# The up projection of a feed-forward layer as a Strassen product of halves, with weight sums made by accumulating transfers

## The chip, the cores and the metric

The kernel runs on one core of one Trainium2 chip. A core has five engines with an instruction stream each: TensorE (PE, matrix products, with its weight loads shown as PEld), VectorE (DVE), ScalarE (ACT), GpSimd (POOL) and SyncE (SP, which here issues most of the DMA transfers). They meet at semaphores. Operands lie in SBUF, products accumulate in PSUM, weights come from HBM by DMA. The metric is the device time of one execution in microseconds; the time before is the median of three runs.

## The reference, cut to what matters

One layer of a hybrid block: a mixer (HGRN2 and mLSTM heads), a residual with layer norm, cross-attention to a memory, a residual with layer norm (LN2), a feed-forward part with a causal convolution, a residual with layer norm. 512 tokens, width 1024, feed-forward width 2816, all in float32. The change lies in the feed-forward part:

```python
def conv_ffn(x, w_up, conv_w, conv_b, w_down):
    u = causal_dwconv(x @ w_up, conv_w, conv_b)     # 512x1024 @ 1024x5632, then 3 taps along the tokens
    gate, val = jnp.split(u, 2, axis=-1)
    return (jax.nn.gelu(gate) * val) @ w_down
...
        x = layer_norm(ALPHA * x + ca, ln2_g[l], ln2_b[l])
        ff = conv_ffn(x, ffn_w_up[l], ffn_conv_w[l], ffn_conv_b[l], ffn_w_down[l])
        x = layer_norm(ALPHA * x + ff, ln3_g[l], ln3_b[l])
```

## The kernel before

Every large product is made in three passes: each float32 operand is split on the chip in a high part (a cast to the matmul format) and a low part (the rest), and `mm3` (L153 to L156) issues high by high (L154), high by low (L155) and low by high (L156) into one PSUM bank. `split` (L118 to L126) splits a block of weights 128 x 1024: a cast on ACT (`wh`, L124), a subtraction on DVE (`wl`, L125), in four buffers each.

The order of work on PE, ACT and DVE is set by a planner inside the kernel's framework, which orders each engine's stream by the program order and its estimate of what is ready; the engines then run their streams in that order, and wait at semaphores. GpSimd and SyncE work in the order in which the instructions are written.

The part before the up projection is the second half of the product with `ca_wo` (by `slab`). For each of four token blocks it adds the residual (`resid`, L658, with the statistics at L660), normalizes (LN2: L664, L422 and L423 for the inverse root, L671 and L673) and transposes the block (`transpose_block`, L252 on PE, then a split out of PSUM: cast at L243 on ACT, subtraction at L244 on DVE) into `x2h` and `x2l`. The transposes of the last block are held back (`x2_last`).

The up projection runs over 22 pairs, each a tile of 128 gate columns and the tile of 128 value columns that belongs to it. A tile is `col_tile`: eight steps along the width by three passes, 24 matmuls with 512 tokens as columns. The first two pairs (`early`) run in two halves of 256 tokens, with `x2_last` between them, so that PE has work on the first tokens while LN2 of the last block ends. `ffn_finish` takes a pair's two banks: `conv3` (a scaled copy with bias on ACT at L793, two DVE operations at L795 for the other taps), the gelu (L802), gate times value (L803), and the split of the result into `hTh` and `hTl` (L804 on ACT, L805 on DVE). The down projection is `slab` twice over the 22 k steps, two at a time, for four token blocks each, and ends with LN3 and the stores.

Names in the profile are those of the tiles: `raw` is a block of weights as loaded, `wh` and `wl` its parts, `fc` a convolved tile, `mm` and `mx` PSUM banks.

## Time and profile before

| | us |
|---|---|
| median of three runs | 819.92 (819.73 to 820.85) |
| the profiled execution | 819.77 |
| its span, first to last instruction | 818.1 |
| its mean granted TensorE clock | 0.995 of full |
| up projection, from its first matmul | 448.57 to 690.00 |
| down projection | 690.00 to 811.00 |
| end (LN3 and stores) | 811.00 to 818.10 |

The span is cut in stretches by the first matmul of each stage. In a view by windows a row gives the stretch, its length, the busy time of PE, PEld, DVE, ACT and POOL with the number of instructions, the granted clock of TensorE, the share of time in which the 16 DMA engines worked, and GB/s. In a timeline a row gives the start, the duration, engine, line, operation, and what it writes from what; a matmul's duration overlaps the next one's, so the length of a step is the distance of two starts. In a view by groups the numbers behind the bar are the busy time of all, the mean of one in ns, and the idle time before them with its releaser.

### The profile page before, as it was taken

The page shows a single profiled execution, that of the slowest core. Times are in us where ns is not written, and L with a number is a line of the kernel's source. Part 1 is how long each engine was busy: PE and PEld are TensorE (multiplying, and loading weights), DVE is VectorE, ACT ScalarE, POOL GpSimd, SP SyncE. Part 2 cuts the span into 40 slices and gives each one's busy share as a digit, 9 for nine tenths or more (in the row PEclk, how much of TensorE's full clock was granted, in tenths as well). Part 3 has the DMA queues.
Part 4 walks back from the last instruction along what each step waited for, and adds up shares of the span by engine and source line. Part 5 has one row for each costly group of instructions (what it writes and reads, how often), then busy time and mean ns, then how long its engine had stood idle before and what let it go on. Part 6 is the DMA issues. An engine that isn't in the chain of part 4 may idle for free.

```text
span 818.1 us, 10034 instructions
## 1 busy us (share of the span) xinstructions
PE 801.5 (98%) x4000; PEld 674.0 (82%) x4000; DVE 504.9 (62%) x863; ACT 318.8 (39%) x434; POOL 30.2 (4%) x52
## 2 busy tenths in 40 slices
PE   8989999999999999999999999999999999999996
PEld 6868887777789888888988988888888888888885
DVE  6563397899787488348548676665566556224237
ACT  3289553353344225237413354444444444222110
POOL 2000100100200010000001000000000000000001
PEclk9999999999999999999999999999999999999998
DMA  8726423135119316321311552223333322142102
GB/s 268 199 72 184 119 79 55 52 81 177 65 52 340 124 52 224 106 84 52 102 58 47 156 154 82 87 89 103 103 104 103 103 99 77 57 154 82 48 1 103
DMA packets 86263, 87.86 MB, mean 107 GB/s; under 512 B 3140, under 2 KB 65732, under 8 KB 86216
## 3 DMA queue, kind: packets, MB, share of 16 engines
q1 hardware_dynamic: 85632, 84.58, 33.6%
q10 hardware_dynamic: 584, 2.64, 0.9%
q8 instruction: 31, 0.51, 0.2%
q14 instruction: 16, 0.13, 0.1%
HBM read 85.10 MB, written 2.12 MB: 107 GB/s over the span
## 4 chain that ended last, share of the span: by engine, by line
PE 88%; DVE 5%; DMA 4%; POOL 1%; issue 1%; ACT 0%; SPq 0%; DVEq 0%; ACTq 0%; POOLq 0%
PE mm L154 27%; PE mm L155 27%; PE mm L156 27%; DMA raw<-in_w_in_dram 3%; PE mx L574 1%; DMA binb<-in_b_in_dram 1%; PE mx L586 1%; PE mx L252 1%; PE mx L464 1%; POOL ss L423 1%; DMA raw<-in_x_t_dram 1%; PE mx L465 1%; PE mx L154 0%; DVE wl L125 0%; PE mx L156 0%
## 5 line engine op out<-in xcount | busy, mean ns | idle before, releaser
L125 DVE TENSOR_TENSOR wl<-raw,wh 128x1024 fp32r<-128x1024 f32 x134 | 163.2, 1221 | 230.3 <-ACT wh L124 229.7
L124 ACT CAST wh<-raw 128x1024 fp32r<-128x1024 f32 x134 | 140.7, 1052 | 242.8 <-PE mm L156 133.0
L154 PE MATMUL mm<-x2h,wh 128*128 128x512 f32 (+1 forms) x384 | 142.8, 372 | 0.0
L155 PE MATMUL mm<-x2l,wh 128*128 128x512 f32 (+1 forms) x384 | 142.6, 371 | 0.0
L156 PE MATMUL mm<-x2h,wl 128*128 128x512 f32 (+1 forms) x384 | 142.6, 371 | 0.0
L155 PEld LDWEIGHTS mm<-x2l,wh 128*128 128x128 f32 x384 | 72.4, 188 | 12.5
L156 PEld LDWEIGHTS mm<-x2h,wl 128*128 128x128 f32 x384 | 72.4, 188 | 12.5
L154 PEld LDWEIGHTS mm<-x2h,wh 128*128 128x128 f32 x384 | 72.4, 188 | 12.3
L155 PE MATMUL mm<-wl,hTh 128*128 128x512 f32 (+1 forms) x198 | 72.4, 366 | 0.0
L154 PE MATMUL mm<-wh,hTh 128*128 128x512 f32 (+1 forms) x198 | 72.4, 366 | 0.0
L795 DVE SCALAR_TENSOR_TENSOR fc<-mm,cols,fc 128x511 f32<-128x511 f32 x88 | 65.6, 746 | 1.5
L156 PE MATMUL mm<-wh,hTl 128*128 128x512 f32 (+1 forms) x180 | 65.8, 365 | 0.0
L154 PE MATMUL mm<-wh,xTh 128*128 128x512 f32 x128 | 51.5, 402 | 0.8 <-DVE xTh L282 0.8
L155 PE MATMUL mm<-wl,xTh 128*128 128x512 f32 x128 | 51.2, 400 | 0.6 <-DVE wl L283 0.5
L156 PE MATMUL mm<-wh,xTl 128*128 128x512 f32 x128 | 50.8, 397 | 0.7 <-DVE xTl L284 0.6
L156 PE MATMUL mm<-xTh,wl 128*128 128x512 f32 x128 | 51.1, 399 | 0.0
L154 PE MATMUL mm<-xTh,wh 128*128 128x512 f32 x128 | 51.1, 399 | 0.0
L155 PE MATMUL mm<-xTl,wh 128*128 128x512 f32 x128 | 51.0, 398 | 0.0
L154 PEld LDWEIGHTS mm<-wh,hTh 128*128 128x128 f32 x198 | 37.4, 189 | 6.2
L155 PEld LDWEIGHTS mm<-wl,hTh 128*128 128x128 f32 x198 | 37.4, 189 | 6.1
L156 PEld LDWEIGHTS mm<-wh,hTl 128*128 128x128 f32 x180 | 33.9, 189 | 5.4
L804 ACT CAST hTh<-fc 128x512 fp32r<-128x512 f32 x22 | 13.7, 620 | 55.7 <-DVE fc L803 55.7
(265 smaller groups left out, 1387.9 us busy)
## 6 DMA issues: line engine op xcount, KB each, us to landing
raw<-in_ffn_w_up_dram SPq DMA_DIRECT2D x44, 512.0 KB, 4.8
raw<-in_w_in_dram SPq DMA_DIRECT2D x14, 1024.0 KB, 8.5
raw<-in_ffn_w_down_dram SPq DMA_DIRECT2D x10, 1024.0 KB, 4.8
...
```

The costliest lines, as they stand in the source:

```text
L124: A.copy(hv, src)
L125: V.tensor_sub(lv, src, f32(hv))
L154: T.matmul(ps, ah, bh, start=first, stop=False, skip_group_check=True)
L155: T.matmul(ps, ah, bl, start=False, stop=False, skip_group_check=True)
L156: T.matmul(ps, al, bh, start=False, stop=last, skip_group_check=True)
L252: T.transpose(ps[:, i * P:(i + 1) * P], src[:, k * P:(k + 1) * P], ident)
L423: G.tensor_tensor(out_, out_, neghalf[:, 0:n], op=OP.pow)
L464: T.matmul(at[:, s], ke[:, s], qe[:, s], start=True, stop=True, skip_group_check=True)
L465: T.matmul(at[0:CH, b * P + CH:(b + 1) * P], kxe[:, b, :], qbo[:, b, :], start=True, stop=True, skip_group_check=True)
L574: T.matmul(ps[:, 0:LEN[j]], kT_[:, j * P:(j + 1) * P], qT_[:, j * P:], start=True, stop=True)
L795: V.scalar_tensor_tensor(y[:, s:], ps[:, :S - s], col(FCW + (2 - s) * 44 + ft), y[:, s:], op0=OP.mult, op1=OP.add)
L804: A.copy(kslice(hTh, i), g)
```

## The change

The product of the up projection is made by Strassen's scheme (in Winograd's form) on halves. The tokens and the width of x are halved, which makes A11, A12, A21, A22, and of each weight tile B the width (rows) and the column tiles are halved: two neighbouring pairs form a quad, whose two gate tiles and two value tiles are the column halves. Eleven quads take the place of 22 pairs. Each quad is seven products instead of eight: one of seven forms of x (A11, A12, A22 and four sums S1 to S4), each 256 tokens by 512 of the width, with one of seven weight blocks (three as loaded, four sums). Each product is 24 matmuls with 256 columns for four of the width's tiles and both gate and value (`product`, L863).

The forms of x are made once, in `forms_block` (L794), which takes the place of `transpose_block` for LN2: blocks 0 and 1 give A11 and A12, blocks 2 and 3 the other five (DVE L811 to L814, the splits at L247). The weight sums r1 to r4 are made by DMA transfers from GpSimd that add to what is in place (`up_forms`, L844, `add` at L848), in a ring of seven blocks of 512 KB. The host lays the weights out so that each such block is contiguous. Products that belong to one result accumulate in one bank; the rest is added by DVE (`put`, L884) with a bank copied out by ACT (`kept`, L880). The convolution then reads SBUF, and gate times value is written in float32 to `hf`; its split into `hTh` and `hTl` moves to the down part (`h_split`, L939, called by `slab`). The tiles `wh` and `wl` are 1152 wide, of which the up weights use the 1024 from column 16 on; the two vectors of a layer norm share one tile; a negated copy of the convolution's columns is made in the head.

```diff
-    def split(src, shape):
-        h = wp.tile([P, 1024], F32R, name="wh", tag="wh", bufs=4)
-        l = wp.tile([P, 1024], F32R, name="wl", tag="wl", bufs=4)
+    def split(src, shape, skew=0):
+        h = wp.tile([P, 1152], F32R, name="wh", tag="wh", bufs=4)[:, skew:skew + 1024]
+        l = wp.tile([P, 1152], F32R, name="wl", tag="wl", bufs=4)[:, skew:skew + 1024]
...
+            if pre:
+                pre(k0)
...
+        gb = H8(F32, "lngb")
+        ln_gb["g"], ln_gb["b"] = gb[:, 0:D], gb[:, D:2 * D]
+        nc.sync.dma_start(ln_gb["g"], bcast(g, D))
+        nc.sync.dma_start(ln_gb["b"], bcast(b_, D))
...
-    x2h = [X8(F32R, "x2h") for _ in range(2)]
-    x2l = [X8(F32R, "x2l") for _ in range(2)]
...
+    forms = {}
+    for n in ("A11", "A12", "S4", "S3", "S2", "S1", "A22"):
+        t = X8(F32R, "xf").rearrange("p (o k t) -> p o k t", o=2, k=4)
+        forms[n] = t[:, 0], t[:, 1]
+    q4t = lambda t: [t.rearrange("p (o k t) -> p o k t", o=2, k=4)[:, i] for i in range(2)]
+    raws = [X8(F32, "xfr") for _ in range(3)]
+    (fA21, fS3), (fS1, fS2), (fA11, fA12) = (q4t(t) for t in raws)
+    fS4 = fA11
+    def forms_block(b):
+        s = slice((b % 2) * P, (b % 2 + 1) * P)
+        ps = []
+        for j in range(2):
+            pj = mx_bank()
+            for i in range(4):
+                k = 4 * j + i
+                T.transpose(pj[:, i * P:(i + 1) * P], xres[b][:, k * P:(k + 1) * P], ident)
+            ps.append(pj.rearrange("p (k t) -> p k t", k=4))
+        put = lambda n, src: split_evict(src, forms[n][0][:, :, s], forms[n][1][:, :, s])
+        c = lambda t: t[:, :, s]
+        if b < 2:
+            for n, pj, raw in (("A11", ps[0], fA11), ("A12", ps[1], fA12)):
+                put(n, pj)
+                A.copy(c(raw), pj)
+            return
+        A.copy(c(fA21), ps[0])
+        V.tensor_sub(c(fS1), ps[1], c(fA21))
+        V.scalar_tensor_tensor(c(fS2), c(fS1), -1.0, c(fA11), op0=OP.mult, op1=OP.subtract)
+        V.tensor_sub(c(fS3), c(fA11), c(fA21))
+        V.scalar_tensor_tensor(c(fS4), c(fS2), -1.0, c(fA12), op0=OP.mult, op1=OP.subtract)
+        for n, src in (("S4", fS4), ("S3", fS3), ("S2", fS2), ("S1", fS1)):
+            put(n, c(src))
+        put("A22", ps[1])
...
     def ln2_evict(b, ps):
         resid(b, ps, 512, 1024)
         norm(b)
-        return lambda: transpose_block(xres[b], b, x2h, x2l)
+        return lambda: forms_block(b)
...
+    hf = [raws[2]] + [H8(F32, "hf") for j in range(5)]
+    def hslice(i):
+        return hf[i // 4][:, (i % 4) * 512:(i % 4 + 1) * 512]
...
+    blocks = [q2.tile([P, 1024], F32, name="rawx")]
+    for _ in range(3):
+        r = wp.tile([P, 2048], F32, name="raw", tag="raw", bufs=3)
+        blocks += [r[:, 0:1024], r[:, 1024:2048]]
+    def up_forms(q, order):
+        blk = lambda kh, ch: ffn_w_up[q, kh, ch]
+        at = {n: blocks[(4 * q + i) % 7] for i, n in enumerate(order + ("T1",))}
+        r1, r2, r3, r4 = (at[n] for n in ("B11", "B22", "B21", "T1"))
+        load, add = nc.sync.dma_start, lambda d, s_: nc.gpsimd.dma_start(d, s_, accum_op=OP.add)
+        src = {"B11": blk(0, 0), "B22": blk(1, 1), "B21": blk(1, 0)}
+        for n in order:
+            load(at[n], src[n])
+        for n in order:
+            yield split(at[n], (8, P), 16)
+            if n == "B22":
+                add(r2, blk(0, 1))
+        load(r4, blk(0, 0))
+        add(r4, blk(0, 1))
+        add(r1, r2)
+        add(r3, r1)
+        for r in (r2, r1, r4, r3):
+            yield split(r, (8, P), 16)
+    def product(bank, n, u, first, last):
+        (h, l), (fh, fl) = u, forms[n]
+        for j in range(2):
+            for k in range(4):
+                mm3(bank[:, j * 256:(j + 1) * 256], h[:, 4 * j + k, :], l[:, 4 * j + k, :], fh[:, k, :], fl[:, k, :],
+                    first and j == 0 and k == 0, last and j == 1 and k == 3)
+    def quad(q):
+        early = q < 2
+        us = up_forms(q, ("B11", "B21", "B22") if early else ("B22", "B11", "B21"))
+        uu = (hf[3 + q] if early else raws[q % 2]).rearrange("p (c j t) -> p c j t", c=2, j=2)
+        g2 = lambda t: t.rearrange("p (j t) -> p j t", j=2)
+        t1, t2_ = slice(0, 256), slice(256, 512)
+        def kept(bank, name):
+            t = t2(name)
+            A.copy(t, bank)
+            return g2(t)
+        def put(dst, bank, other):
+            V.tensor_tensor(dst, g2(bank), other, op=OP.add)
+        def third():
+            b = mx_bank()
+            product(b, "S4", next(us), True, True)
+            return kept(b, "m3")
+        if not early:
+            m3 = third()
+        bp = mm_bank()
+        product(bp, "A11", next(us), True, False)
+        m1 = kept(bp, "m1")
+        b = mx_bank()
+        product(b, "A12", next(us), True, True)
+        put(uu[:, 0, :, t1], b, m1)
+        if early:
+            yield
+            m3 = third()
+        b4 = mm_bank()
+        product(b4, "S3", next(us), True, False)
+        m7 = kept(b4, "m7")
+        product(bp, "S2", next(us), False, False)
+        u2 = kept(bp, "u2")
+        product(bp, "S1", next(us), False, True)
+        put(uu[:, 1, :, t1], bp, m3)
+        put(uu[:, 1, :, t2_], bp, m7)
+        product(b4, "A22", next(us), False, True)
+        put(uu[:, 0, :, t2_], b4, u2)
+        for c in (1, 0):
+            y = []
             for j in range(2):
+                ft = j * NPAIR + 2 * q + c
+                u, f = uu[:, c, j, :], t2("fc")
+                w = lambda i: ncols[:, i * 44 + ft:i * 44 + ft + 1] if c else col(FCW + i * 44 + ft)
+                A.activation(f, u, AF.Identity, bias=col(FCB + ft), scale=w(2))
+                for d in (1, 2):
+                    V.scalar_tensor_tensor(f[:, d:], u[:, :S - d], w(2 - d), f[:, d:], op0=OP.mult, op1=OP.add)
+                y.append(f)
+            A.activation(y[0], y[0], AF.Gelu_apprx_tanh)
+            V.tensor_mul(hslice(2 * q + c), y[0], y[1])
+    early = [quad(q) for q in range(2)]
+    next(early[0])
+    x2_last()
+    next(early[1])
+    for g in early:
+        for _ in g:
+            pass
+    for q in range(2, NQ):
+        for _ in quad(q):
+            pass
...
+    def h_split(k):
+        j, c = k // 4, k % 4 * 512
+        if c == 0:
+            if j < 5:
+                hTh.append(X8(F32R, "hTh"))
+                hTl.append(X8(F32R, "hTl"))
+            else:
+                hTh.append(H8(F32R, "hTr"))
+                hTl.append(hTh[5][:, 1024:])
+        s = slice(c, c + 1024)
+        A.copy(hTh[j][:, s], hf[j][:, s])
+        V.tensor_sub(hTl[j][:, s], hf[j][:, s], f32(hTh[j][:, s]))
     slab(tok(hTh), tok(hTl), ffn_w_down[0], 0, NPAIR, lambda b, ps: resid(b, ps),
-         mid=lambda: ln_load(ln3_g, ln3_b))
+         mid=lambda: ln_load(ln3_g, ln3_b), pre=h_split)
...
+    a["ffn_w_up"] = (a["ffn_w_up"][0].reshape(2, 4, P, 2, NQ, 2, P).transpose(4, 0, 5, 2, 3, 1, 6)
+                     .reshape(NQ, 2, 2, P, 1024))
```

The instruction order moves at three places. The first is DVE around LN2 of the last token block (`xres3`), before:

```order
L244 TENSOR_TENSOR x2l_3533<-mx_3725,x2h_3531 128x4x128 [waits Activation_49]
L660 BN_STATS st24_3526<-xres3_2222 128x6 [waits DVE_49]
L660 BN_STATS st24_3526<-xres3_2222 128x6
L125 TENSOR_TENSOR wl_3770<-raw_3766,wh_3769 128x1024 [waits DMAHW6_49]
L664 BN_AGGR lnmv_3735<-st24_3526 128x2 [waits DVE_49]
L125 TENSOR_TENSOR wl_3774<-raw_3766,wh_3773 128x1024 [waits DMAHW7_49]
L422 TENSOR_SCALAR lnrs_3737<-lnmv_3735 128x1 [waits DVE_49]
L671 SCALAR_TENSOR_TENSOR xres3_2222<-xres3_2222,lnmv_3735,lng_2223 128x512 x2
L673 SCALAR_TENSOR_TENSOR xres3_2222<-xres3_2222,lnrs_3737,lnb_2224 128x512 [waits DVE_49,Pool_49]
L673 SCALAR_TENSOR_TENSOR xres3_2222<-xres3_2222,lnrs_3737,lnb_2224 128x512 [waits DVE_49]
L244 TENSOR_TENSOR x2l_3532<-mx_3853,x2h_3530 128x4x128 [waits Activation_49]
L244 TENSOR_TENSOR x2l_3533<-mx_3860,x2h_3531 128x4x128 [waits Activation_49]
```

and of the changed kernel (`xfr` and `xf` are the float32 and split forms of x, `hf` the target of a quad's first sum, `lngb` the merged norm vectors):

```order
L664 SCALAR_TENSOR_TENSOR xres3_2224<-xres3_2224,mm_3545 128x512 [waits PE_49]
L126 TENSOR_TENSOR wl_3812<-raw_3773,wh_3811 128x1024 [waits DMAHW3_49,Activation_49]
L811 TENSOR_TENSOR xfr_3540<-mx_3735,xfr_3539 128x4x128 [waits PE_49,Activation_49]
L813 TENSOR_TENSOR xfr_3539<-xfr_3541,xfr_3539 128x4x128
...
L126 TENSOR_TENSOR wl_3870<-raw_3774,wh_3869 128x1024 [waits DMAHW7_49]
L247 TENSOR_TENSOR xf_3534<-xfr_3541,xf_3534 128x4x128 [waits Activation_49]
...
L884 TENSOR_TENSOR hf_3769<-mx_3810,m1_3808 128x2x256 [waits PE_49]
L427 TENSOR_SCALAR lnrs_3760<-lnmv_3758 128x1 [waits DVE_49]
L677 SCALAR_TENSOR_TENSOR xres3_2224<-xres3_2224,lnmv_3758,lngb_3461 128x512 x2
```

Between the residual (L664 now, L658 before) and the norm of the last block stand the four sums of forms (of which the first two are shown), five splits of forms (the first is shown) and a sum of products; before there were two splits of x and three of weights.

The second place is GpSimd's stream, before (LN2's and LN3's inverse roots, nothing between them):

```order
L423 TENSOR_TENSOR lnrs_3637<-lnrs_3637,neghalf_104 128x1 [waits DVE_49,Pool_49]
L423 TENSOR_TENSOR lnrs_3687<-lnrs_3687,neghalf_104 128x1 [waits DVE_49,Pool_49]
L423 TENSOR_TENSOR lnrs_3737<-lnrs_3737,neghalf_104 128x1 [waits DVE_49,Pool_49]
L423 TENSOR_TENSOR lnrs_6113<-lnrs_6113,neghalf_104 128x1 [waits DVE_49,Pool_49]
L423 TENSOR_TENSOR lnrs_6151<-lnrs_6151,neghalf_104 128x1 [waits DVE_49,Pool_49]
```

and of the changed kernel from LN2's last inverse root on, where each row L848 is one adding transfer, onto the block named first (the blocks of the ring are `rawx` and the halves of three `raw`):

```order
L428 TENSOR_TENSOR lnrs_3760<-lnrs_3760,neghalf_104 128x1 [waits DVE_49,Pool_49]
L848 DMA raw_3773<-in_ffn_w_up_dram 128x1024 [waits DMAHW4_49,DMAHW5_49,DMAHW2_49,DMAHW7_49,DVE_49,Activation_49]
L848 DMA rawx_3772<-raw_3773 128x1024 [waits DMAHW7_49,DMASW1_49,PE_49]
L848 DMA raw_3773<-rawx_3772 128x1024 [waits DMAHW3_49,DMASW2_49]
L848 DMA raw_3775<-in_ffn_w_up_dram 128x1024 [waits DMAHW7_49,DMAHW2_49,DVE_49]
L848 DMA rawx_3772<-in_ffn_w_up_dram 128x1024 [waits DMAHW5_49]
L848 DMA raw_3774<-raw_3775 128x1024 [waits DMAHW7_49,DMASW4_49]
```

The first is r2 of quad 0, the second adds it to r1, the third adds that to r3, and each waits for the one before (DMASW is the count of GpSimd's transfers, DMAHW that of SyncE's). The first also waits for the split of its block on ACT and DVE. The fourth is r2 of quad 1, the fifth r4 of quad 0.

The third place is DVE in the steady part of the up projection; before, one pair:

```order
L125 TENSOR_TENSOR wl_4380<-raw_4376,wh_4379 128x1024 [waits DMAHW4_49,PE_49,Activation_49]
L795 SCALAR_TENSOR_TENSOR fc_4291<-mm_4241,cols_106,fc_4291 128x511 [waits Activation_49]
L795 SCALAR_TENSOR_TENSOR fc_4291<-mm_4241,cols_106,fc_4291 128x510 [waits DVE_49]
L125 TENSOR_TENSOR wl_4384<-raw_4376,wh_4383 128x1024 [waits DMAHW5_49,PE_49,Activation_49]
L795 SCALAR_TENSOR_TENSOR fc_4295<-mm_4242,cols_106,fc_4295 128x511 [waits Activation_49]
L795 SCALAR_TENSOR_TENSOR fc_4295<-mm_4242,cols_106,fc_4295 128x510 [waits DVE_49]
L803 TENSOR_TENSOR fc_4291<-fc_4291,fc_4295 128x512 [waits DVE_49]
L805 TENSOR_TENSOR hTl_3751<-fc_4291,hTh_3745 128x512 [waits Activation_49]
```

and of the changed kernel the end of one quad and the beginning of the next:

```order
L884 TENSOR_TENSOR xfr_3540<-mm_5097,u2_5160 128x2x256 [waits PE_49]
L126 TENSOR_TENSOR wl_5309<-raw_3775,wh_5308 128x1024 [waits DMAHW5_49,Activation_49]
L920 SCALAR_TENSOR_TENSOR fc_5221<-xfr_3540,ncols_275,fc_5221 128x511 [waits Activation_49]
...
L923 TENSOR_TENSOR hf_3768<-fc_5221,fc_5225 128x512 [waits DVE_49,Activation_49]
L920 SCALAR_TENSOR_TENSOR fc_5231<-xfr_3540,cols_106,fc_5231 128x510 [waits DVE_49]
L920 SCALAR_TENSOR_TENSOR fc_5235<-xfr_3540,cols_106,fc_5235 128x511
L126 TENSOR_TENSOR wl_5343<-raw_3774,wh_5342 128x1024 [waits DMASW1_49]
L920 SCALAR_TENSOR_TENSOR fc_5235<-xfr_3540,cols_106,fc_5235 128x510 [waits DVE_49]
L884 TENSOR_TENSOR xfr_3539<-mx_5307,m1_5305 128x2x256 [waits PE_49,Activation_49]
L923 TENSOR_TENSOR hf_3768<-fc_5231,fc_5235 128x512 [waits DVE_49]
L126 TENSOR_TENSOR wl_5373<-raw_3774,wh_5372 128x1024 [waits DMASW2_49]
```

Two splits of weights stood between convolution steps; now the convolution of a quad (eight steps, of which the last are shown) stands as one group ahead of the splits of the weight sums (those that wait for DMASW).

## Rows read from the trace of the kernel before

**Rows 1.** Page, busy time, share of the span, instructions of each engine
```profile
PE 801.5 (98%) x4000; PEld 674.0 (82%) x4000; DVE 504.9 (62%) x863; ACT 318.8 (39%) x434; POOL 30.2 (4%) x52
```

**Rows 2.** Page, chain that ended last, share of each engine
```profile
PE 88%; DVE 5%; DMA 4%; POOL 1%; issue 1%; ACT 0%; SPq 0%; DVEq 0%; ACTq 0%; POOLq 0%
```

**Rows 3.** Windows by stage: length; PE, PEld, DVE, ACT, POOL; clock, DMA share, GB/s
```profile
448.57:690.00 241.43, 241.43 (x1163) 204.09 (x1162) 151.88 (x188) 104.70 (x135) 0.92 (x1) 1.00 0.35 105
...
690.00:811.00 121.00, 121.00 (x596) 102.62 (x594) 45.34 (x64) 21.33 (x21) 2.75 (x3) 1.00 0.22 73
```

**Rows 4.** Timeline, PE, up projection: start, duration, engine, line, operation
```profile
539.67 0.39 PE L156 MATMUL mm<-x2h,wl 128*128 128x512 f32 x1
...
542.84 0.39 PE L155 MATMUL mm<-x2l,wh 128*128 128x512 f32 x1
```

**Rows 5.** Timeline, PE, first pairs of the up projection
```profile
448.77 0.28 PE L155 MATMUL mm<-x2l,wh 128*128 128x256 f32 x1
...
457.17 0.28 PE L156 MATMUL mm<-x2h,wl 128*128 128x256 f32 x1
457.29 1.04 PE L252 MATMUL mx<-ident,xres 128*128 128x128 f32 x8
```

**Rows 6.** Tile x2h, one line: duration min/median/max, first and last start, forms
```profile
L154 PE MATMUL mm<-x2h,wh x384: 278/389/396, 448.6 to 689.5; 128*128 128x512 f32 x160, 128*128 128x256 f32 x32
```

**Rows 7.** Timeline, DVE, around the end of LN2
```profile
449.11 1.22 DVE L125 TENSOR_TENSOR wl<-raw,wh 128x1024 fp32r<-128x1024 f32 x1
450.24 1.28 DVE L244 TENSOR_TENSOR x2l<-mx,x2h 128x512 fp32r<-128x512 f32 x2
451.44 0.74 DVE L660 BATCH_NORM_STATS2 st<-xres 128x6 f32<-128x256 f32 x2
...
454.53 1.40 DVE L671 SCALAR_TENSOR_TENSOR xres<-xres,lnmv,lng 128x512 f32<-128x512 f32 x2
455.86 1.40 DVE L673 SCALAR_TENSOR_TENSOR xres<-xres,lnrs,lnb 128x512 f32<-128x512 f32 x2
```

**Rows 8.** Groups of DVE by form: busy us, mean ns of one
```profile
L125 DVE TENSOR_TENSOR wl<-raw,wh 128x1024 fp32r<-128x1024 f32 x134 | 163.2, 1221 | 230.3 <-ACT wh L124 229.7 <-PE mx L574 0.3
...
L803 DVE TENSOR_TENSOR fc<-fc 128x512 f32<-128x512 f32 x22 | 15.2, 692 | 0.9
```

**Rows 9.** Groups of ACT by form
```profile
L124 ACT CAST wh<-raw 128x1024 fp32r<-128x1024 f32 x134 | 140.7, 1052 | 242.8 <-PE mm L156 133.0 <-PE mm L155 79.7 <-DVE xres L658 13.2
...
L793 ACT ACTIVATE fc<-mm,cols 128x512 f32<-128x512 f32 x44 | 34.1, 775 | 0.0
...
L802 ACT ACTIVATE fc<-fc 128x512 f32<-128x512 f32 x22 | 13.9, 632 | 42.5 <-DVE fc L795 42.5
...
L395 ACT ACT_TABLE_LOAD x4 | 5.1, 1283 | 0.1
...
L243 ACT CAST x2h<-mx 128x512 fp32r<-128x512 f32 x8 | 4.3, 588 | 23.4 <-PE mx L252 23.4
```

**Rows 10.** DMA view, issues: count, KB each, median us to landing
```profile
raw<-in_ffn_w_up_dram SPq DMA_DIRECT2D x44, 512.0 KB, 4.8
...
out_dram<-xres SPq DMA_DIRECT2D x8, 256.0 KB, 2.0
...
raw<-in_ffn_w_down_dram SPq DMA_DIRECT2D x2, 512.0 KB, 3.9
```

**Rows 11.** Page, DMA queues: packets, MB, share of 16 engines
```profile
q1 hardware_dynamic: 85632, 84.58, 33.6%
q10 hardware_dynamic: 584, 2.64, 0.9%
```

**Rows 12.** Windows of 5 us
```profile
50.00:55.00 5.00, 1.49 (x10) 0.94 (x8) 2.62 (x9) 3.38 (x5) 0.00 (x0) 1.00 0.03 4
55.00:60.00 5.00, 5.00 (x16) 3.96 (x16) 2.64 (x5) 4.54 (x6) 0.00 (x0) 0.66 0.02 3
```

**Rows 13.** Waits of PE: us in total, times, longest
```profile
PE mx L376 <- ACT ae L371: 3.5, 1, 3.5
```

65 lines of the change are left out of this document (13 added, 52 removed).

## The prediction

> **What bounds the kernel now.** I read the page's busy times first: TensorE (PE) is busy for 98% of the span, VectorE (DVE) for 62%, ScalarE (ACT) for 39% [rows 1]; then the chain that ended last, of which 88% is PE [rows 2]. So PE bounds, and a change gains what it takes off PE and loses what it makes PE wait. Then the stretches. From 448.57 to 690.00 us, the up projection, PE is busy for the whole 241.43 us; DVE for 151.88, ACT for 104.70, the DMA engines at a share of 0.35. The down projection follows at the same full PE, with DVE at 45.34 of 121.00 [rows 3]. Nothing is idle on PE there, so everything outside PE was free, and the question is whether it stays free.
>
> Two step lengths carry the sum. With 512 columns, 14 steps from 539.67 to 542.84 make 0.2264 us each [rows 4]. With 256 columns, 70 steps from 448.77 to 457.17 make 0.120 us each [rows 5]; half the columns cost 53%, not half. That those are the 256-column steps of the two first pairs shows in the tile view of x2h: of 192 matmuls of this line on that buffer 160 have 512 columns and 32 have 256, the first of them at 448.6 us [rows 6].
>
> **PE's share of the change.** Before: 2 pairs in halves, 192 steps of 0.120 (23.0), and 20 pairs of 48 steps of 0.2264 (217.3): 240.4 us, with 0.9 for the last eight transposes 241.3, which is the stretch. After: 11 quads of 7 products of 24 steps, 1848 steps of 0.120: 221.8 us. The removal of an eighth of the multiplications is thus worth 18.6 us and not 30, because the narrower step is dearer. Without any wait up would end at 671.3 and the run at about 801.
>
> **The other engines in a quad of 20.16 us (168 steps).** DVE: seven weight splits at the spacing of 1.14 (449.11 to 450.24 [rows 7]; 1221 ns by its group [rows 8]), four sums out of PSUM at 0.60 (half the stretch of L244's pair, 450.24 to 451.44 [rows 7]), eight convolution steps at 0.66 (half of L671's pair, 454.53 to 455.86 [rows 7]), two products at 0.62 (an estimate just under the 692 ns of L803 [rows 8]): 8.0 + 2.4 + 5.3 + 1.2 = 16.9 us. ACT: seven casts of 1.0, four copies of 0.59 (the x2h cast out of PSUM), four convolution starts at 0.78 (L793), two gelus of 0.63 [rows 9]: 14.8. Both fit, but DVE's load goes from 63% to 84%, and its order is fixed: the last sum of a quad, the split of the third loaded block, the eight convolution steps and only among them the split of the weight sum for S3 of the next quad. By the order I count 0.2 to 0.5 us of slack before S3 and S2. I take a loss of 0.2 per quad; none to 1.0 is the bound, the upper one being one late split.
>
> **The start of the stage.** PE has the same order as before until 448.57. Then come three products of 24 steps (to 457.2), and the transposes of the last token block. Before, these waited for nothing: DVE ended LN2 at 455.86 + 1.40 = 457.26, just in time for 457.29 [rows 5, 7]. Now DVE's row holds the forms of block 2 ahead of LN2's end: four sums (4 x 0.66) and five splits (4 x 0.62 and one more from PSUM at 0.60) and one sum of products (0.60), against two splits (1.2) and one weight split (1.14) that leave: +4.1 us. LN2 ends at 461.3, PE waits some 3.3 us (the transposes could start at 458.0). After the transposes PE has one product (to 465.1), while ACT copies the block and DVE makes its forms (a copy, four sums, five splits, one sum of products: 0.59 + 2.64 + 3.1 + 0.6), and then splits the block B22: 469.8. PE waits another 4.5 us before S4 of quad 0. Together 7.8 us that before did not exist.
>
> **The adds.** Only when B22 is split may GpSimd issue the add that makes r2 of quad 0 in its place. The two that follow (r1 of r2, r3 of r1) each wait for the one before. Call L the time from issue to landing of one such add. PE then waits L - 0.4 before S3, L - 2.6 before S2, L - 2.3 before A22 (between them stand products of 2.9 us; part of A22 is ordered ahead of S1, so S1 hides nothing for it): 3L - 5.3. In quad 1 the convolution of quad 0 and a table load (1283 ns, as ACT shows elsewhere [rows 9]) stand ahead of its splits, and r4's add ahead of r1's in GpSimd's queue: about 3 us before S2 and 3 before A22 more. Without waits quad 2 would begin at 448.57 + 0.9 + 14 x 2.88 = 489.8; with them at 489.8 + 7.8 + (3L - 5.3) + 5.9.
>
> L is not in this trace: before, all data went through two queues that hardware feeds, none through GpSimd's [rows 11], and none added. The nearest rows are plain loads: 512 KB in 3.9 us (down weights) and 4.8 us (up weights), 256 KB in 2.0 [rows 10]. Below, L could be near 2.5, if the fixed part is small and only the plain rate counts (512 KB at the 256 KB row's rate is 4.0; the wide rows of 4 KB that the new layout brings may go faster); above, an add reads two operands, so twice 3.9: 7.8. I take 5, nearest to the plain rows with something for the second operand. The Trainium skill, "DMA: Bandwidth & Descriptors", section on the anatomy of one DMA on the SWDGE path, gives such a transfer a constant of about 2.0 us plus its bytes at 436 GB/s, and "Collectives: The Full Stack", on why ReduceScatter is half of AllGather, says an add in the transfer costs a second source read: 2.0 + 2 x 1.2 = 4.4 us as an estimate, by which my sum would be 2 us less. The trace here shows neither.
>
> With L = 5: 489.8 + 7.8 + 9.7 + 5.9 = 513.2. Nine quads of 20.16 and 0.2 each: 183.2, so up ends at 696.4, 6.4 us later than before.
>
> **In the steady quads** the adds lie far ahead: r2 must land some 20.5 us after its source was split, with splits that is L up to about 6; r1 allows 7.7, r3 7.1. At L = 5 all are hidden. Each us beyond costs up to three per quad. Transfers: eight per quad, four of them with two reads, 6.3 MB in 20.2 us or 312 GB/s. The stretch of before moved 105 GB/s at a share of 0.35 [rows 3], so 300 at a full share: little is left, and this is the ground for a longer L than the plain rows. (Counting a second read as the same work is an assumption.)
>
> **Clock.** The granted clock is full all through before, but after 3.5 us in which PE waited for ACT (50 to 55 us, busy for 1.49 of 5) the next 5 us ran at 0.66, a mix of the two levels 2.4 and 1.2 GHz [rows 12, 13]. The waits at the start are of that length. Most of a slow stretch would lie in the waits themselves; I add one stretch, 5 x 0.34 = 1.7 us.
>
> **The down part** takes over 11 splits of gate times value, 1.14 each on DVE and 1.05 on ACT. A unit of two k steps lasts 24 x 0.2264 = 5.4 us on PE, and DVE is at 37% there [rows 3]; each split lies beside a unit. I cost it at nothing; the first one uncovered would cost 2.2. The merged LN vectors and the negated columns (one small operation in the head) are nothing too.
>
> **Sum.** 6.4 + 1.7 = +8.1 on the profiled execution of 819.77 (span 818.1 and 1.7 around it; the median of the runs is 819.92, the same within 0.15): 827.9, so 828 us.
>
> **Rivals.**
> A. The adds are quick, or the start hides more. L = 2.5 gives 489.8 + 7.8 + 2.2 + 4.1 (less in quad 1 too) = 503.9 and, without the 0.2 and the clock, an end at 685.3: 815. With half of the 7.8 us of forms gone too: 811. For it: 4 KB rows; the forms are cheap in small. Against it: the serial chain is in the order, and 3.9 us is the quickest 512 KB that the trace has.
> B. The adds are slow and contend, from L = 7 on. At 7.8 the start costs 489.8 + 7.8 + 18.1 + 9 = 524.7, the quads each some 2 us: 724 at the end of up, 854 in all. It decides above L = 7.1, where r3 is late in each quad. For it: 312 GB/s against some 300 at full share. The Trainium skill, "SBUF — State Buffer", section with the "DVE blocks DMA" trap, says that VectorE in a two-port mode keeps GpSimd from writing descriptors; that would hold an add back by up to one DVE instruction, 1.2 us; no run here shows it.
> C. DVE is the bound in the quads: its 16.9 us wait on ACT and PE in turns, and each quad loses 1 us: 828 + 7 = 835. Against it: 3.3 us of slack in the sum. It decides where the splits for S3 and S2 come late.
> D. The two sides cancel: L near 3.5 gives a start of quad 2 at 508.0 and an end of 689.4: 819 to 821, no change.
>
> **Chances.** Forecast (L 4 to 6.5, small losses: 821.6 to 834) 0.42; A 0.27; B 0.12; C 0.07; D 0.12. Within 0.2% (818.3 to 821.6), about what a measurement of this kernel can tell from no change: 0.12. Slower 0.61, faster 0.27. The range, with a tenth left out at each end, goes from 812 to 852; the forecast's own is 822 to 834.
>
> **What would show it.** Right: PE idle before the last transposes (3 us), before S4 (4 to 5), S3, S2 and A22 of quad 0 released by DMA; steps of 0.120; quads of 20.2 to 20.5 us; adds of 4 to 6 us. Wrong: adds under 3.5 us or over 7, quads above 21 us released by DVE or ACT, steps away from 0.120, a wait at the beginning of the down part, or no wait before the transposes.

## The result and the profile after

The changed kernel takes 872.68 us (870.29 to 873.29, four runs) against 820.18 for the one before in the same comparison: a ratio of 1.0634, 95% interval 1.0612 to 1.0656. Slower, as forecast, but by 52 us and not by 8; 828 with a range of 812 to 852 missed it. The profiled execution took 872.24 us with a span of 870.5.

The page, busy times and DMA queues (q0 is GpSimd's, which [rows 11] did not have):

```profile
PE 806.2 (93%) x4696; PEld 709.3 (81%) x4696; DVE 570.4 (66%) x944; ACT 376.3 (43%) x512; POOL 68.3 (8%) x96
...
q0 software_dynamic: 6336, 23.07, 14.3%
```

Windows by stage (columns as in [rows 3]): the start, that is up to the first product of quad 2, then quads 2 to 10, the down projection, and the end:

```profile
451.17:521.40 70.23, 51.14 (x348) 48.29 (x347) 43.23 (x60) 29.55 (x41) 8.79 (x10) 0.83 0.52 122
521.40:742.50 221.10, 193.16 (x1514) 189.42 (x1513) 158.38 (x193) 122.19 (x159) 29.39 (x34) 0.92 0.71 169
742.50:863.40 120.90, 120.89 (x596) 102.49 (x594) 59.91 (x81) 29.56 (x31) 2.78 (x3) 1.00 0.25 86
863.40:870.50 7.10, 0.00 (x0) 0.00 (x0) 3.91 (x8) 0.00 (x0) 0.92 (x1) 0.72 0.27 100
```

PE, full for all of the stage in [rows 3], now waits, and its clock is at 0.83 and 0.92. The down projection is unchanged at 120.9 us with the 11 splits in it. In quads 2 to 10 PE is idle for 27.9 of 221.1 us; its 1512 steps at the length below would take 172.7 us, so another 20.5 us went into steps at the lower clock.

Two steps of the timeline of PE in the first product of the up projection, 20 steps apart:

```profile
451.60 0.28 PE L155 MATMUL mm<-xf,wh 128*128 128x256 f32 x1
...
453.87 0.28 PE L157 MATMUL mm<-xf,wl 128*128 128x256 f32 x1
```

2.27 us for 20 steps, 0.1135 each; over the stage the mean of the undisturbed ones is 0.1142. [Rows 5] had 0.120. So PE's own time for a quad is 19.2 us, not 20.16.

What PE waits for (total, times, longest), and the transfers of the up weights (SPq are the loads, POOLq the adds; median us to landing):

```profile
PE mm L157 <- DVE wl L126: 32.1, 12, 4.5
PE mm L155 <- ACT wh L125: 8.1, 3, 4.6
PE mx L381 <- ACT ae L376: 5.8, 1, 5.8
PE mx L801 <- DVE xres L679: 3.1, 1, 3.1
```

```profile
raw<-in_ffn_w_up_dram SPq DMA_DIRECT2D x37, 512.0 KB, 4.5
...
raw<-in_ffn_w_up_dram POOLq DMA_DIRECT2D x19, 512.0 KB, 8.6
...
raw<-raw POOLq DMA_DIRECT2D x15, 512.0 KB, 4.7
```

An add out of SBUF takes 4.7 us, near the 5 assumed; one out of HBM 8.6.

One steady quad. GpSimd's issues (idle time and its releaser in brackets): r2 at 588.90, r1 at 598.69, r3 at 603.83, r4 at 610.67, the next r2 at 613.53:

```profile
588.90 0.86 POOL L848 DMA_DIRECT2D raw<-in_ffn_w_up_dram  x1 [0.56 <-DVE wl L126]
598.69 0.87 POOL L848 DMA_DIRECT2D rawx<-raw  x1 [8.93 <-issue]
603.83 0.87 POOL L848 DMA_DIRECT2D raw<-rawx  x1 [4.27 <-DVE fc L920]
610.67 0.85 POOL L848 DMA_DIRECT2D raw<-in_ffn_w_up_dram  x1 [5.97 <-DMA raw<-in_ffn_w_up_dram]
613.53 0.86 POOL L848 DMA_DIRECT2D raw<-in_ffn_w_up_dram  x1 [2.01 <-DVE wl L126]
```

ACT beside it:

```profile
598.14 1.05 ACT L125 CAST wh<-raw 128x1024 fp32r<-128x1024 f32 x1 [3.31 <-DMA raw<-in_ffn_w_up_dram]
599.10 1.52 ACT L918 ACTIVATE fc<-xfr,cols,ncols 128x512 f32<-128x512 f32 x2
...
608.68 1.05 ACT L125 CAST wh<-raw 128x1024 fp32r<-128x1024 f32 x1 [2.48 <-DMA raw<-rawx]
610.81 1.05 ACT L125 CAST wh<-raw 128x1024 fp32r<-128x1024 f32 x1 [1.08 <-PE mm L156]
```

and DVE and PE:

```profile
599.94 2.78 DVE L920 SCALAR_TENSOR_TENSOR fc<-xfr,ncols,fc 128x511 f32<-128x511 f32 x4 [3.00 <-ACT fc L918]
...
605.23 1.22 DVE L126 TENSOR_TENSOR wl<-raw,wh 128x1024 fp32r<-128x1024 f32 x1
...
611.89 1.23 DVE L126 TENSOR_TENSOR wl<-raw,wh 128x1024 fp32r<-128x1024 f32 x1 [0.18 <-ACT wh L125]
```

```profile
603.17 0.28 PE L156 MATMUL mm<-xf,wh 128*128 128x256 f32 x1
606.50 0.39 PE L157 MATMUL mm<-xf,wl 128*128 128x256 f32 x1 [3.05 <-DVE wl L126]
```

Two chains can be read here. Chain A is the adds in series: r2 9.79 us, r1 5.14, r3 4.85 until ACT casts r3 (608.68), and only behind that, in ACT's order, the cast of the next quad's B22 (610.81), its subtraction (611.89), and the next r2 (613.53): 24.63 us, the length of a quad, of which ACT waits 1.08 us for a weight buffer that S3 gives back. Chain B is the convolution: ACT's order has r2's cast ahead of the convolution's start, so that starts when r2 has landed; DVE's order has seven of its eight steps ahead of r2's split, which ends at 606.45, 8.3 us after the cast began. PE's third step of S3 waits for that (606.50). Chain B closes through that weight buffer: r2's add until its cast 9.24 us (598.14), the cast, the convolution and the subtraction 8.31 (606.45), S3, mostly at the lower clock, until it gives the buffer back 4.36 (610.81), and B22's split until the next r2 2.72 (613.53), which is 24.63 again, without slack. Waits of ACT for such a buffer and of PE in S3, from 521.4 to 742.5 us (quads 2 to 10):

```profile
ACT wh L125 <- PE mm L156: 7.2, 6, 1.6
...
PE mm L157 <- DVE wl L126: 27.3, 9, 4.5
```

In six of the eight turns from quad to quad the cast of the next B22 waits for S3's buffer, 0.4 to 1.6 us, so that chain B binds there and chain A has that much to spare; in the other two it follows r3's cast at once. r2's add stands in both chains. What each is worth, the experiments say.

### The profile page after: what moved, and what is told of

Same layout as the page of the kernel before. It is cut to its first block, busy times and chain, and to the rows that moved or that the text cites. A ratio compares the mean times of both kernels' runs of the same rounds, so it can differ in the third digit from the quotient of the medians.

```text
span 870.5 us, 11772 instructions
## 1 busy us (share of the span) xinstructions
PE 806.2 (93%) x4696; PEld 709.3 (81%) x4696; DVE 570.4 (66%) x944; ACT 376.3 (43%) x512; POOL 68.3 (8%) x96
## 3 DMA queue, kind: packets, MB, share of 16 engines
q0 software_dynamic: 6336, 23.07, 14.3%
## 5 line engine op out<-in xcount | busy, mean ns | idle before, releaser
L126 DVE TENSOR_TENSOR wl<-raw,wh 128x1024 fp32r<-128x1024 f32 x155 | 187.4, 1221 | 172.3 <-ACT wh L125 171.6
L125 ACT CAST wh<-raw 128x1024 fp32r<-128x1024 f32 x155 | 161.7, 1051 | 311.3 <-PE mm L157 126.2
L157 PE MATMUL mm<-xf,wl 128*128 128x256 f32 x440 | 133.0, 303 | 32.2 <-DVE wl L126 32.1
L155 PE MATMUL mm<-xf,wh 128*128 128x256 f32 x440 | 133.4, 304 | 8.9 <-ACT wh L125 8.1
L156 PE MATMUL mm<-xf,wh 128*128 128x256 f32 x440 | 131.0, 299 | 0.0
L157 PEld LDWEIGHTS mm<-xf,wl 128*128 128x128 f32 x440 | 93.0, 211 | 35.0 <-DVE wl L126 35.0
L155 PEld LDWEIGHTS mm<-xf,wh 128*128 128x128 f32 x440 | 93.1, 212 | 11.4 <-ACT wh L125 8.7
L156 PEld LDWEIGHTS mm<-xf,wh 128*128 128x128 f32 x440 | 92.9, 211 | 0.0
L155 PE MATMUL mm<-wh,hTh 128*128 128x512 f32 (+1 forms) x180 | 65.8, 366 | 0.0
L157 PE MATMUL mx<-xf,wl 128*128 128x256 f32 x176 | 49.4, 280 | 1.9 <-DVE wl L126 1.9
L156 PE MATMUL mx<-xf,wh 128*128 128x256 f32 x176 | 49.5, 281 | 0.8 <-DVE xf L247 0.8
L155 PE MATMUL mx<-xf,wh 128*128 128x256 f32 x176 | 49.9, 284 | 0.2 <-ACT wh L125 0.2
L920 DVE SCALAR_TENSOR_TENSOR fc<-xfr,ncols,fc 128x511 f32<-128x511 f32 (+1 forms) x36 | 25.0, 748 | 24.1 <-ACT fc L918 24.1
```

What stands on the lines that cost most here:

```text
L125: A.copy(hv, src)
L126: V.tensor_sub(lv, src, f32(hv))
L155: T.matmul(ps, ah, bh, start=first, stop=False, skip_group_check=True)
L156: T.matmul(ps, ah, bl, start=False, stop=False, skip_group_check=True)
L157: T.matmul(ps, al, bh, start=False, stop=last, skip_group_check=True)
L920: V.scalar_tensor_tensor(f[:, d:], u[:, :S - d], w(2 - d), f[:, d:], op0=OP.mult, op1=OP.add)
```

## The experiments

To compare quads: from the first matmul of S4 of quad 3 to the last of the up projection are eight quads; the column gives an eighth of it, read from each kernel's timeline of PE.

| kernel | us | one quad |
|---|---|---|
| changed | 872.7 | 24.4 |
| e1 plain copies | 842.0 | 22.3 |
| e2 no add of r4 | 853.7 | 22.2 |
| e3 GpSimd's additions | 866.3 | 24.5 |
| e5 convolution later | 865.6 | 23.1 |
| e9 B22 earlier | 869.6 | 24.9 |
| e10 both moves | 843.6 | 21.2 |
| e7 copies, convolution later | 824.3 | 19.8 |
| e6 GpSimd's additions, convolution later | 872.9 | 25.9 |
| e11 e10, r2 of its own | 840.3 | 21.0 |
| e12 new start | 819.2 | 21.1 |

**e1, e2: the cost of adding, and of r4's add.**

```diff
-        ... lambda d, s_: nc.gpsimd.dma_start(d, s_, accum_op=OP.add)
+        ... lambda d, s_: nc.gpsimd.dma_start(d, s_)          # e1
-        add(r4, blk(0, 1))                                    # e2
```

> The four adding transfers of a quad become plain copies from the same queue at the same places with the same waits, so the weight sums are left out. Theory 1 (a loop of latencies: the block B22 is split only when S3 of the quad before has given a weight buffer back, then r2's add takes 9.4 us, then it is split, then S3 can run): r2's transfer falls to some 5 to 6 us, the quad from 24.6 to about 21, the run from 872 to about 838. Theory 2 (volume: the 16 DMA engines, at a share of 0.7 to 0.8 in the up stage, are the limit): the reads of the targets go, about a third of the work, and the quad falls to PE's own 19.1: about 822. Theory 3 (the splits are late because they stand behind the convolution on VectorE and ScalarE, not because of the adds): the steady quads stay within 1 us of 24.6, about 860 to 872, and only the start is shorter.

842.03 us (840.74 to 843.15), ratio 1.0272 (1.0238 to 1.0306). Without the second read the transfers are 2 us shorter each:

```profile
raw<-in_ffn_w_up_dram POOLq DMA_DIRECT2D x19, 512.0 KB, 6.6
raw<-raw POOLq DMA_DIRECT2D x15, 512.0 KB, 2.9
```

Theory 3 falls as it stood, and theory 2; theory 1 (838, quads of 21) is nearest. Chain A is 6 us shorter by its three transfers, chain B only by r2's, and the quad by 2.1. The trace has chain B as what holds it: the cast of the next B22 waits for S3's buffer nine times from 514.28 to 712.9 us (quads 2 to 10), 2.4 us in the mean:

```profile
ACT wh L125 <- PE mm L156: 21.8, 9, 4.0
```

> The add of r4 alone is left out (its block is loaded, so S1 works with a wrong sum). It is not ahead of S3's weights except in GpSimd's queue and on the DMA engines. Theory 1 with r2's add slow because it runs beside r4's (issued 1.4 to 3.5 us before it): r2 falls from 9.4 to about 6 us, as in quad 0 where it runs alone, the quad to about 21.5, the run to about 845. Theory 1 with r2 slow because of the loads that start with it: r2 stays above 8.5 us, the run at 865 or more. Theory 2 (volume): one of eight transfers goes, the quad falls by 12 percent at most to 21.6. Theory 3: no change, 870.

853.71 us (849.48 to 857.22), ratio 1.0429 (1.0373 to 1.0485), quads of 22.2; the HBM adds, now r2's alone, take 6.5 us at the median in place of 8.6. So r4's add, which GpSimd issues up to 3.5 us ahead of r2's and which is needed later, makes r2 late. (`up_forms` writes r2's add first; in the steady quads GpSimd's stream is thus not in the written order, as was said ahead.) One transfer less is also less volume, for which the expectation allowed 21.6 at the least; e2 alone does not tell the two apart.

**e3, e6: the same sums without DMA.**

```diff
-        load, add = nc.sync.dma_start, lambda d, s_: nc.gpsimd.dma_start(d, s_, accum_op=OP.add)
+        load, add = nc.sync.dma_start, lambda d, s_: G.tensor_tensor(d, d, s_, op=OP.add)
+        load(r4, blk(0, 1))
...
-                add(r2, blk(0, 1))
+                add(r2, r4)
...
-        load(r4, blk(0, 0))
-        add(r4, blk(0, 1))
+        add(r4, r1)
         add(r1, r2)
```

> The same sums, made by GpSimd's own additions (128x1024) out of four plain loads for each quad, in the same ring; B12 is loaded in the slot of r4 in place of B11. No add goes through a DMA. Theories 1 and 2: if one addition takes 2 to 3 us, r2 lands some 7 us earlier, the steady quads fall to 19.1 to 20.2, the DMA share to about 0.4, the start loses 6 to 9 us less, and the run comes to about 805 to 815. Theory 3: the quads stay near 24. If an addition takes more than 4.8 us, GpSimd becomes the bound with four of them in a quad, and the run is above 825; if it slows VectorE's splits, their mean rises above 1.23 us and the quads above 20.5.

866.33 us (865.62 to 867.10), ratio 1.0569 (1.0536 to 1.0603). (The load of quad 1's B12 falls on r1 of quad 0 here, so quads 0 and 1 compute with other sums; e6 has that load later.) The sums are quick, the quads as long as ever. GpSimd, then ACT's cast of r2 and DVE, in one quad:

```profile
582.66 2.40 POOL L848 TENSOR_TENSOR raw<-raw 128x1024 f32<-128x1024 f32 x1 [12.35 <-DVE wl L126]
585.13 3.27 POOL L848 TENSOR_TENSOR raw<-raw,rawx 128x1024 f32<-128x1024 f32 x1
588.48 2.41 POOL L848 TENSOR_TENSOR rawx<-rawx,raw 128x1024 f32<-128x1024 f32 x1
592.11 2.79 POOL L848 TENSOR_TENSOR raw<-raw,rawx 128x1024 f32<-128x1024 f32 x1 [1.22 <-issue]
```

```profile
588.84 1.05 ACT L125 CAST wh<-raw 128x1024 fp32r<-128x1024 f32 x1 [0.21 <-PE mm L156]
...
589.52 2.45 DVE L126 TENSOR_TENSOR wl<-raw,wh 128x1024 fp32r<-128x1024 f32 x1
591.90 4.87 DVE L920 SCALAR_TENSOR_TENSOR fc<-xfr,ncols,fc 128x511 f32<-128x511 f32 x4
...
599.28 1.21 DVE L126 TENSOR_TENSOR wl<-raw,wh 128x1024 fp32r<-128x1024 f32 x1
```

r2 is there at 585.1, and its split still ends at 600.5, behind the convolution. Its cast (588.84) waits not for r2 but for the buffer that A22 gives back, so the convolution holds the quad without any add: from A22's end through the convolution and r2's split to S3 and the next A22. From the cast to the end of the split pass 11.7 us where the changed kernel has 8.3, since DVE's operations beside GpSimd's are slower (a split 2.45 us against 1.22, four convolution steps 4.87 against 2.78).

**e5, e9, e10: cutting chain B, chain A, both.** The convolution of a quad is written behind S3 of the next (e5, e10); the next quad's B22 is split ahead of this quad's r3, with r2's add written right behind that split (e9, e10).

```diff
         m7 = kept(b4, "m7")
+        while later:
+            later.pop()()            # conv() of the quad before; e5, e10
...
+        if 2 <= q + 1 < NQ:          # e9, e10
+            g = up_forms(q + 1, ("B22", "B11", "B21"))
+            ahead[q + 1] = g, next(g)
         product(b4, "A22", next(us), False, True)
```

> The changed kernel with one thing moved: a quad's convolution, gelu and product are written behind the seventh of the next quad that S3 closes, so that on VectorE and ScalarE the splits of the next quad's weight sums stand ahead of them. The adds stay. Theory 3 (the sum for S3 is split only behind the convolution; in the changed kernel 8.3 us passed from r2's landing to the end of its split, against 2.2 for a cast and a subtraction): r2's split ends some 6 us earlier, the 3 us gap before S3 goes with its stretch at half clock, the quad falls from 24.6 to 19.5 to 20.5, the run to 825 to 835. Theory 1 (the add's 9.4 us by themselves set the quad, since S3 frees the buffer that B22's split waits for): the quad stays above 23, the run above 855.

> The changed kernel with one thing moved: the split of the next quad's B22, and with it r2's add, is written ahead of the split of this quad's r3. Theory 4: two loops bind the steady quads at nearly the same length, so that cutting one alone gives little. Loop A: r2's add, r1's, r3's one after the other (9.8 + 5.1 + 4.9 us in the changed kernel), then the splits of r3 and of the next B22 in that order (4.8), which frees the next r2: 24.6. Loop B: the end of A22, the sum of its bank, the convolution, and only then r2's split and the four products S3, S2, S1, A22 (12 + 11 us): 23 to 24. With loop A cut, loop B holds the quads at 22.5 to 24.2, the run at 850 to 868. Theory 1 alone (adds set the quad, the convolution does not): quads 19.5 to 20.5, run 825 to 835.

> Both moves: the convolution behind S3 of the next quad, and the next B22's split ahead of r3's. The adds stay as they are. Theory 4 (two loops): quads of 19.3 to 20.5 us with no gap above 1 us, the run at 826 to 834, near the 824 of the kernel with plain copies and the deferred convolution. Theory 2 (the DMA engines' volume, at a share of 0.72 with quads of 24.6, would need 0.88 with quads of 20): quads stay above 22, the run above 845.

e5: 865.62 us (863.71 to 866.70), ratio 1.0550 (1.0531 to 1.0569), quads of 23.1. e9: 869.57 (867.64 to 871.80), ratio 1.0614 (1.0583 to 1.0646), 24.9, a little above what was expected. Both: 843.59 (838.93 to 844.17), ratio 1.0280 (1.0240 to 1.0321), 21.2. e5 by itself looks like theory 1, e3 and e9 like theory 3. So 7 us and 3 us apart and 29 together: no single chain binds, and the longest of several sets the quad. With chain B cut, chain A holds e5.

e9 is not held by the convolution alone, as loop B of its expectation had it. r2's split, then SyncE's load of the next r4, GpSimd's adds of r4 and r2, and r1's:

```profile
601.20 1.22 DVE L126 TENSOR_TENSOR wl<-raw,wh 128x1024 fp32r<-128x1024 f32 x1
...
602.49 0.33 SPq L857 DMA_DIRECT2D raw<-in_ffn_w_up_dram  x1
...
609.10 1.74 POOL L848 DMA_DIRECT2D raw<-in_ffn_w_up_dram  x2 [6.30 <-DMA raw<-in_ffn_w_up_dram]
622.57 0.86 POOL L848 DMA_DIRECT2D raw<-raw  x1 [11.73 <-issue]
```

The next r4 is loaded into r2's block, hence only when r2 has been split (602.42), and GpSimd holds the next r2 behind r4's add (both from 609.10). This is a chain C: r2's add, its split behind the convolution, r4's load, the next r2. And with r4's add 1.0 us ahead of r2's in the mean, in place of 2.5, r2 takes longer: from its issue to r1's pass 11.5 us in the mean, against 9.7 in the changed kernel. The move cut two chains and lengthened a third.

For both moves 826 to 834 was expected; the quads came out 0.7 over the upper end, and the start only 3 us shorter. Windows of e10, start and quads 2 to 10:

```profile
451.65:518.70 67.05, 49.37 (x338) 46.37 (x337) 39.46 (x56) 28.27 (x40) 7.90 (x10) 0.85 0.50 117
518.70:713.50 194.80, 181.21 (x1522) 176.57 (x1521) 159.41 (x193) 122.49 (x160) 30.19 (x35) 0.99 0.79 193
```

The DMA engines move more per us than in the changed kernel (193 GB/s at a share of 0.79, against 169 at 0.71), so volume was not what held the quads at 24.6. With the gaps gone the clock is at 0.99: of the 26.3 us that quads 2 to 10 lose, 14.3 are PE's idle time (27.9 to 13.6) and 12.0 its slow steps. What holds e10 at 21.2 was not tried. Its trace has chain C again, with r1's add in place of the convolution:

```profile
576.25 0.86 POOL L848 DMA_DIRECT2D raw<-in_ffn_w_up_dram  x1 [0.41 <-DVE wl L126]
586.94 0.87 POOL L848 DMA_DIRECT2D rawx<-raw  x1 [9.82 <-DVE wl L126]
592.23 0.33 SPq L857 DMA_DIRECT2D raw<-in_ffn_w_up_dram  x1
596.38 0.85 POOL L848 DMA_DIRECT2D raw<-in_ffn_w_up_dram  x1 [2.77 <-DMA raw<-in_ffn_w_up_dram]
597.71 0.86 POOL L848 DMA_DIRECT2D raw<-in_ffn_w_up_dram  x1 [0.47 <-DVE wl L126]
```

r2 10.69 us, r1 5.29 until it has read r2's block, r4's load into that block 4.15, and the next r2 1.33 behind r4: 21.46, a quad. A block of its own for r4, or r4's add behind r2's, is the next thing to try.

> Plain copies in place of the adds (the sums left out) with the deferred convolution: what remains without the second read. Theory 3 alone: within 4 us of the same kernel with adds, that is only the start is shorter. Theories 1 and 3 together: 8 or more us faster than it, quads at 19.1.

824.33 us (823.67 to 824.60), ratio 1.0048 (1.0033 to 1.0063), quads of 19.8 at a clock of 1.00, 41 us faster than e5. With the convolution out of the way, the length of the adds decides: theories 1 and 3 together.

> The sums by GpSimd's additions (as before, with the load of B12 for quad 1 behind quad 0's sums) and the deferred convolution. The quad with GpSimd's additions alone was 24.4 us although r2 was there 2.4 us after its source was split, so its loop can't be the add's time. Theory 3: quad 19.1 to 20, all waits at the start only; with a start that loses some 7 us less than the adds by DMA, 815 to 825. Theory 1 has no reason for a gain here: 860. VectorE's splits beside GpSimd's additions took up to 2.45 us in place of 1.22; if that counts, the quads stay at 21 or more.

872.94 us (871.21 to 874.24), ratio 1.0635 (1.0614 to 1.0655), quads of 25.9: a miss. GpSimd's additions are no gain here either, and the windows say why: in quads 2 to 10 DVE is busy for 224.33 of 235.10 us, where the changed kernel has 158.38 of 221.10. Slowed by GpSimd as in e3, DVE itself has become the bound.

```profile
507.60:742.70 235.10, 195.28 (x1514) 189.74 (x1513) 224.33 (x195) 122.30 (x160) 100.67 (x35) 0.92 0.23 79
```

**e4, e8: the place of the weights in SBUF.**

```diff
-            yield split(at[n], (8, P), 16)       # e8; e4 puts the 1152 wide tiles and 16 into the kernel before
+            yield split(at[n], (8, P), 0)
```

> The kernel before with only the weight tiles of the changed one: 1152 wide, and for the up projection the 1024 columns from 16 on. In the changed kernel a step of 256 columns took 0.1136 us, in the one before 0.120. Theory A (the place of the weights in SBUF makes the difference): the 192 steps of 256 columns fall to 0.1136, and the 512 column steps of the up part from 0.2264 to about 0.220, so the up part is 241.4 - 1.2 - 6 and the run about 813. Theory B (it is the layout of x or the bank, not the weights): steps unchanged, 820 within 0.2 percent.

> The changed kernel with the weights of the up projection at column 0 of the 1152 wide tiles, not 16. Theory A (their place in SBUF sets the step): steps of 256 columns go from 0.114 to 0.119 to 0.121 us, as in the kernel before, so 1848 steps cost 9 to 12 us more of PE; since the quads wait for other things, less of it shows, 872 to 880. Theory B (no effect): 872, steps 0.114.

e8: 873.57 us (869.52 to 875.14), ratio 1.0642 (1.0612 to 1.0672); its undisturbed steps are 0.1198 us, so the 16 columns are worth 5% of a 256-column step here, and the waits swallowed it. e4: 827.36 (824.30 to 829.19), ratio 1.0085 (1.0052 to 1.0118), the wrong way: its 512-column steps went from 0.2267 to 0.2333, its 256-column ones only from 0.120 to 0.118, and the longer head (below) adds to it. One place does not suit both shapes.

**e11, e12: the start.** e11 builds r2 of the two early quads in a block of its own. e12 also makes quad 0 by eight plain products, with A21 and A22 split ahead of the sums of the forms.

```diff
+        if q == 0:                               # e11; for the early quads r4 then takes B22's block
+            load(r2, blk(0, 1))
+            add(r2, blk(1, 1))
...
+    half(0, ("A11", "A12"), slice(0, 256), A.copy)      # e12: quad 0, each half() two products
+    x2_last()
+    half(1, ("A11", "A12"), slice(0, 256), A.copy)
+    for r in rests:                              # the sums S1 to S4 of the forms
+        r()
+    half(0, ("A21", "A22"), slice(256, 512), A.copy)
+    half(1, ("A21", "A22"), slice(256, 512), A.copy)
```

> As the kernel with both moves, and in the two early quads r2 is built in a block of its own (B12 loaded, B22 added), so that it does not wait for B22's split, r4 in B22's block, and A22 stands ahead of S1. Only the start changes: the waits before S3, S2 and A22 of quads 0 and 1 were 5.2, 2.9, 1.2 and 4.3 us in the changed kernel by its trace; if they are the adds' chain behind B22's split, 7 to 11 us go, and the run comes to 8 us under the kernel with both moves, 817 to 824. If the start is set by VectorE's forms instead, less than 3 us go.

> Both moves in the steady quads, and a new start: the first quad is made by eight plain products with the blocks as loaded (one product more, no sums, a split form of A21 added), of which four need only the first half of the tokens, so that six products lie ahead of the last transposes in place of three to four; of the forms of the second half of the tokens A21 and A22 are split first and the four sums after the last transposes; quad 1 has r2 in a block of its own. If the start's 25 to 30 us of waits (quad 2 began at 516 to 521 in the kernels so far, against 490 by PE's own steps) are the adds behind the forms, quad 2 begins at 494 to 500, the steady quads take 20.5 to 21, and up ends at 680 to 688: 810 to 819, at or under the 820 of the kernel before. If VectorE's forms and splits bind the start instead, quad 2 begins at 508 or later and the run stays at 826 or more.

e11: 840.26 us (837.34 to 842.51), ratio 1.0254 (1.0222 to 1.0285), 3 us less than e10, with runs that overlap (837.34 to 842.51 and 838.93 to 844.17), where 8 were expected: the adds alone are not the start. e12: 819.19 (815.61 to 821.50, 12 runs) against 820.77, ratio 0.9975 (0.9959 to 0.9990). Its windows, quads 0 and 1, and the rest:

```profile
452.12:499.60 47.48, 46.24 (x397) 45.84 (x396) 38.00 (x56) 28.43 (x42) 6.33 (x7) 1.00 0.67 167
499.60:690.30 190.70, 178.58 (x1488) 174.56 (x1487) 156.03 (x189) 120.70 (x157) 29.70 (x34) 0.98 0.78 191
```

Expected were 810 to 819, with quad 2 at 494 to 500. PE is idle for 1.2 us of the start in place of 19.1, with one product more, and the waits before the transposes and S4 are gone; which of the moves in it did that was not separated. This version is a quarter of a per cent under the kernel before, so the scheme can pay, by little: a quad of 21.1 us against two pairs of 2 x 48 x 0.2264 = 21.7.

## Why the prediction was wrong

That the kernel would be slower was right, the place was not: the forecast lost its time in the start of the stage, and most of the measured loss lies in the steady quads. In the order of the prediction's steps, from the traces of both kernels:

- **The head, taken as nothing:** the up projection begins 2.6 us later (451.17 against 448.57). It is there before any add: PE waits 5.8 us at the transposes behind `ae` where [rows 13] had 3.5. e4, which shares the wide weight tiles and nothing else with the change, has it too (5.4, and its up projection begins at 451.97); why they cost this was not tried.
- **PE's share, right in kind:** 1848 steps, but of 0.1142 and not 0.120; the gain that waits hide is 29, not 19 us.
- **The other engines, about right:** 16.9 us of DVE in a quad were forecast and 17.6 measured (158.38 by 9). ACT's terms add up to 13.7 and not to the 14.8 given, and 13.6 were measured; DVE's "+4.1" at the start adds up to 4.0. No other term hangs on these slips.
- **The start, near, by errors that partly cancel:** LN2 late by the forms (PE waits 3.1 us, forecast 3.3); r2's add of quad 0 issued at 472.56, forecast 469.8 and 2.6 for the head; 6.3 and 4.9 us between issues where L was taken as 5. (The fifth row of GpSimd's stream shown ahead is r4 of quad 1; that of quad 0 is issued at 425.63.) In all PE is idle for 19.1 us of the start where 7.8 + 9.7 + 5.9 = 23.4 were forecast, but it is busy for 51.14 us with what takes 39.3 at full clock (336 steps and the transposes), so some 12 went into slow steps where 1.7 was set down. Quad 2 begins at 521.4; 513.2 and 2.6 were forecast, so 5.6 more.
- **The steady quads, the step that failed:** "At L = 5 all are hidden", with 0.2 us lost per quad. Forecast 183.2 us, measured 221.1: 37.9 of the 44.3 us that separate 827.9 from 872.24 (head 2.6, start 5.6, less the 1.7 set down for the clock). Two errors meet there. The first is the size of a term: L was one number, 5, for two kinds of add. Out of SBUF it measured 4.7; r2's, out of HBM beside r4's add and three loads, took 8.4 to 9.9 from its issue to its cast, over the prediction's own limit for it of about 6. The second is a wait left out: the adds were held against limits counted from a split of B22 (about 6, 7.7 and 7.1), but what has to end before that split had no term. The next B22 stands behind r3 in ACT's order and behind S3's weight buffer, so that a late r2 makes the next one late, and the whole turn has to stay under a quad: 9.8 + 5.1 + 4.9 + 4.8. With L = 5 throughout it would have been 3 x 5 + 4.8 = 19.8, about PE's quad already, so r2's size decided and the closed turn made it count in every quad. That the cast of the next B22 stands right behind r3's in ACT's order could be read before the run. Rival B had the price (L at 7.8), and its ground, the share of the DMA engines, was not what held the quads (e10); its chance of 0.12 was too small, and its 2 us per quad too low (24.6 against 20.2).
- **r2's split:** 0.2 to 0.5 us of slack were counted before S3; from the beginning of r2's cast to the end of its split 8.3 us passed, and PE waited for it 27.3 us in nine quads. The order told that it stands among the convolution's steps; that the convolution's start in turn stands behind r2's cast on ACT, so that neither runs while r2 is on its way, was missed.
- **The clock:** one slow stretch of 1.7 us was put down; quads 2 to 10 alone lost 20.5. Eight of the nine gaps before S3's third step, 2.6 to 4.8 us from step to step, were followed by steps at the lower of the two levels. Windows of the changed kernel, before S3's gap, the gap, and the steps behind it:

```profile
598.00:603.10 5.10, 5.10 (x48) 5.10 (x47) 3.16 (x5) 4.89 (x7) 0.87 (x1) 1.00 0.55 106
603.10:606.50 3.40, 0.35 (x5) 0.15 (x3) 3.40 (x6) 3.00 (x4) 0.87 (x1) 1.00 0.40 77
...
607.00:610.50 3.50, 3.50 (x20) 3.50 (x19) 3.50 (x6) 1.05 (x1) 0.00 (x0) 0.53 0.67 191
```

  This gap costs its length and, at half the clock, half as much again (3.5 us at 0.53); in all, 27.9 us of idle time brought 20.5 us of slow steps. That it recurs from quad to quad was the thing to see; [rows 12] had shown the price once.
- **The down part, right:** 120.9 us against 121.0 in [rows 3], with the splits hidden.
